# Recurrence of a two-block transformer on one core: block-diagonal products as pairs of array tiles

## The chip, the cores and the metric

The kernel runs on one core of a Trainium2 chip. The metric is device time in microseconds: the median of three runs was 2415.47 us (2414.92 to 2416.41). Besides these runs one execution was profiled, with 2423.21 us; its instructions span 2421.4 us. All rows below are of that execution.

## The reference, cut to what matters

The program is a stack of two blocks on 256 tokens of width 1024, all in float32. The first block's first token mixer is a bidirectional RWKV-7: 16 heads of width 64, a forward and a backward direction, and per head and direction the recurrence

```
state = state * w_t + sa * b_t + v_t * k_t        # state 64 x 64, sa = state . a_t
y_t   = state . r_t
```

over the 256 tokens. Everything before it (norms, projections, decay and gate) and everything after it (group norm of y, output projection, mixture of experts with 32 experts, then a dilated attention, a second mixture of experts, and a second model with two layers of its own) is not touched by the change.

## The kernel before

The recurrence is computed in chunks of 64 tokens. A job is one direction (z) and two heads (hp = 0, 1), named by et = 0 to 7; so there are 16 jobs, each with 2 heads x 4 chunks. Two chunks lie side by side on the 128 partitions: chunk c = 2 tt + cp, with cp = 0 on partitions 0 to 63 and cp = 1 on 64 to 127 (`rows(cp)`). The pair of a head and of a pair of chunks is q = 2 hp + tt. A tile such as `mq[:, q, s]` is 128x128 and block-diagonal: a 64x64 block for cp = 0 in the upper left, one for cp = 1 in the lower right, and zeros elsewhere. MQB (four such matrices per q), LGK (three) and ZZ are set to zero once, and only the diagonal blocks are written later.

A job goes through these steps; after each `yield` the next generator gets its turn:

- L1113: inner products of b, k with a, r, one 64x64 array tile per head and chunk; each head has a PSUM tile of its own (`psa[hp]`). VectorE multiplies them by masks into MQB (L1119) and LGK (L1121); L1123 puts inverses of 16x16 blocks into `mq[:, :, 1]`.
- Twice (lv = 0, 1), to extend the inverse from blocks of 16 to 32 and then 64: transposes of `mq[:, q, 1]` (L1137), copied by ScalarE into Mt (L1141); product of `mq[:, q, 0]` and Mt (L1147); VectorE masks it into Z (L1149); product of Z and `mq[:, q, 1]` (L1167); VectorE adds it (L1169). At lv = 0 there are also transposes (L1155, L1175), the product of `lg_[:, q, 0]` and v (L1162), and ScalarE's copies of them (L1156, L1164, L1178).
- L1183: the inverse times AW, four products of 128x128 by 128x128 into one PSUM tile; ScalarE copies the result to UW (L1186).
- L1194 and L1198, "the last ones": UW times `mq[:, q, 2:4]` (i = 1 into pw, i = 0 into py) and v times `lg_[:, q, 1:3]` added into py. The contraction runs over both chunks, and since the right-hand matrices are block-diagonal a product has 256 columns: s = 0, 1 times two chunks. VectorE adds pw into RA (L1202, L1203); ScalarE copies py to YH (L1205).
- Then `across` starts as a generator of its own: the state goes from chunk to chunk (L1221 transpose, L1223 copy, L1226 product, L1229 and L1230 adds), and at its end `norm` is appended after every second et.

`roundrobin` takes turns between two chains of jobs (one per direction, each with its own MQB, LGK, SB and ZZ), the `across` and `norm` generators, and `side`, which loads and multiplies the modulation weights of both layers (L1849, products of 128x32 array tiles by 512 columns). PSUM has two tags of four tiles each ("b", "c"), a tile being one bank. The order of the instructions on each engine comes from this order of emission and from the framework's scheduler, which can bring an independent instruction forward. Every f32 product shows as two records in the profile, a transpose as one.

When the recurrence is done, `tail` opens more buffers for weights, and the loads of the output projection and of the experts follow.

Of the kernel before, what the change touches and what calls it, by code (L numbers as in the profile page):

```python
# [20 lines left out]
F32 = mybir.dt.float32  # L21
F32R = mybir.dt.float32r
I32 = mybir.dt.int32
AF = mybir.ActivationFunctionType
OP = mybir.AluOpType
AX = mybir.AxisListType
P = 128
# [677 lines left out]
def rwkv(N, src, I, cst, emit, side, tail, scratch):  # L705


    nc, tc = N.nc, N.tc
    v, g, sc = nc.vector, nc.gpsimd, nc.scalar
# [4 lines left out]
    rows = lambda h: slice(h * 64, h * 64 + 64)  # L714
# [13 lines left out]
    o = 0  # L728
# [41 lines left out]
    for tt in range(NT):  # L770
        src.norm(tt)
        for k4 in range(2):
            ps = N.psum("b")
            for kk in range(4):
                nc.tensor.transpose(ps[:, kk * P:(kk + 1) * P], src.tok(tt, 4 * k4 + kk), N.ident)
            o, pk = hc[:, 4 * k4:4 * k4 + 4, tt * P:(tt + 1) * P], ps.rearrange("p (k t) -> p k t", k=4)
# [55 lines left out]
    for i, dst in ((0, hw), (1, ha)):  # L832
        xs = shifted(3 + i)
        ps = N.psum("b")
# [10 lines left out]
    ps = N.psum("b")  # L845
# [179 lines left out]
    jp = pool("jp", 2, e4s)  # L1025
# [65 lines left out]
    def job(z, et, buf):  # L1091
# [3 lines left out]
        ar = AR[z][e2].rearrange("p s (c t) -> p s c t", t=64)[:, :, 4 * e:4 * e + 4]  # L1095
        pl = PL[z][e2][:, 4 * e:4 * e + 4]
        vz = vt[:, :, et * P:(et + 1) * P]
        if z:
            vz = jp.tile([P, NT, P], F32, tag="vr", name=N.nm("vr"))
            ps = N.psum("c")  # L1100
# [2 lines left out]
            sc.activation(vz, ps[:, 0:256].rearrange("p (t x) -> p t x", t=2), AF.Copy)  # L1103
        mq, lg_, sb = MQB[buf], LGK[buf], SB[buf]
        t4 = lambda a: a.rearrange("p (q t) -> p q t", q=4)
        pairs = [(hp, tt) for hp in range(2) for tt in range(2)]
        psa = [N.psum("b") for _ in range(2)]
        for i, src in ((0, bt), (1, kt)):
            for tt in range(2):
                for hp in range(2):  # L1110
                    for cp in range(2):
                        c = 2 * tt + cp
                        nc.tensor.matmul(psa[hp][rows(cp), (2 * i + tt) * P:(2 * i + tt + 1) * P], c3(src)[rows(hp), c, :],  # L1113
                                         ar[rows(hp), 0:2, c, :], start=True, stop=True)
        for hp in range(2):
            for cp in range(2):
                a = psa[hp][rows(cp), :].rearrange("p (i t s x) -> p i t s x", i=2, t=2, s=2)
                o = mq[rows(cp), 2 * hp:2 * hp + 2, 0::2, cp * 64:cp * 64 + 64]
                v.tensor_mul(o, a[:, 0], m_ni[rows(cp), None, :, :].to_broadcast([64, 2, 2, 64]))  # L1119
                o = lg_[rows(cp), 2 * hp:2 * hp + 2, 0:2, cp * 64:cp * 64 + 64]  # L1120
# [10 lines left out]
        DP = jp.tile([P, 4, 64], F32, tag="DP", name=N.nm("DP"))  # L1131
        g.tensor_mul(DP, eye[:, None, :].to_broadcast([P, 4, 64]), pb)
        AW = jp.tile([P, 4, 2, 64], F32, tag="AW", name=N.nm("AW"))
        for lv in range(2):
# [5 lines left out]
            Mt = jp.tile([P, 4, 64], F32, tag="Mt", name=N.nm("Mt"))  # L1140
# [3 lines left out]
            qbc = lambda a: a.rearrange("p (q b c) -> p q b c", q=4, c=sz)  # L1144
            pz = N.psum("b")
            for q in range(4):
                nc.tensor.matmul(pz[:, q * 64:(q + 1) * 64], mq[:, q, 0, :], Mt[:, q, :], start=True, stop=True)  # L1147
            Z = ZZ[buf][:, lv]
            v.tensor_mul(Z.rearrange("p q (b s c) -> p q s b c", s=2, c=sz)[:, :, 0], qbc(pz[:, 0:256]),  # L1149
                         blk(m_lv[lv], 0)[:, None].to_broadcast([P, 4, 64 // sz, sz]))  # L1150
# [1 line left out]
            if lv == 0:  # L1152
                ps = N.psum("c")
                for tt in range(2):
                    nc.tensor.transpose(ps[:, tt * P:(tt + 1) * P], at[:, tt * P:(tt + 1) * P], N.ident)  # L1155
                sc.activation(AW[:, :, 1, :].rearrange("p (h t) d -> p t h d", h=2),  # L1156
                              ps[:, 0:256].rearrange("p (t h d) -> p t h d", t=2, h=2), AF.Copy)
                pc = N.psum("c")
                for q, (hp, tt) in enumerate(pairs):
                    vh = vz[:, tt, hp * 64:(hp + 1) * 64]  # L1160
                    for cp in range(2):
                        nc.tensor.matmul(pc[rows(cp), q * 64:(q + 1) * 64], lg_[:, q, 0, cp * 64:cp * 64 + 64], vh,  # L1162
                                         start=True, stop=True)
                sc.activation(AW[:, :, 0, :], c3(pc[:, 0:256]), AF.Copy)  # L1164
            pm = N.psum("b")
            for q in range(4):
                nc.tensor.matmul(pm[:, q * 64:(q + 1) * 64], Z[:, q, :], blk(mq[:, q, 1, :], 1), start=True, stop=True)  # L1167
            o = mq[:, :, 1, :].rearrange("p q (b s c) -> p q s b c", s=2, c=sz)[:, :, 1]
            v.tensor_add(o, o, qbc(pm[:, 0:256]))  # L1169
            yield  # L1170
# [9 lines left out]

        pu = N.psum("b")
        for q in range(4):
            nc.tensor.matmul(pu[:, q * P:(q + 1) * P], mq[:, q, 1, :], AW[:, q].rearrange("p s d -> p (s d)"), start=True,  # L1183
                             stop=True)
        UW = jp.tile([P, 4, 2, 64], F32, tag="Z", name=N.nm("UW"))
        sc.activation(UW, pu.rearrange("p (q s d) -> p q s d", q=4, s=2), AF.Copy)  # L1186
        yield

        pw, py = N.psum("c"), N.psum("b")
        for tt in range(2):  # L1190
            for i, ps in ((1, pw), (0, py)):
                for hp in range(2):
                    q = 2 * hp + tt
                    nc.tensor.matmul(ps[rows(hp), tt * 256:(tt + 1) * 256], UW[:, q, i, :], mq[:, q, 2:4, :], start=True,  # L1194
                                     stop=i == 1)
            for hp in range(2):
                q = 2 * hp + tt
                nc.tensor.matmul(py[rows(hp), tt * 256:(tt + 1) * 256], vz[:, tt, hp * 64:(hp + 1) * 64],  # L1198
                                 lg_[:, q, 1:3, :], start=False, stop=True)
        RA = jp.tile([P, 2, 2, 2, 64], F32, tag="RA", name=N.nm("RA"), bufs=3)  # L1200
        w5 = pw.rearrange("p (t s c x) -> p t s c x", t=2, s=2, c=2)
        v.tensor_add(RA[:, :, 0], w5[:, :, 0], ar[:, 1].rearrange("p (t c) x -> p t c x", t=2))  # L1202
        v.tensor_add(RA[:, :, 1], w5[:, :, 1], DP.rearrange("p (t c) x -> p t c x", t=2))  # L1203
        YH = jp.tile([P, 2, 2, 2, 64], F32, tag="YH", name=N.nm("YH"), bufs=3)
        sc.activation(YH, py.rearrange("p (t s c x) -> p t s c x", t=2, s=2, c=2), AF.Copy)  # L1205
        gens.append(across(z, et, buf, RA, YH))
        yield

# [979 lines left out]
```

## Time and profile before

| | |
|---|---|
| median of 3 runs | 2415.47 us |
| profiled execution | 2423.21 us |
| its span | 2421.4 us |
| TensorE busy (share of span) | 2112.9 us (87%) |
| VectorE busy | 1151.2 us (48%) |
| ScalarE busy | 704.8 us (29%) |
| GpSimd busy | 369.3 us (15%) |
| mean granted TensorE clock | 0.92 |

Busy times are unions over the whole span, which has stages with different limits. TensorE's matmul records (PE) have modelled ends and overlap each other, and weight loads (PEld) run beside them; the pace of a queue is read from the starts. The granted clock is a share of full speed.

### The profile page before, as it was taken

How to read it: one execution, taken by the hardware profiler on the slowest of the kernel's cores; microseconds unless marked ns; L12 is line 12 of the kernel's file. 1: busy time of each engine (PE TensorE's matmuls, PEld its weight loads, DVE VectorE, ACT ScalarE, POOL GpSimd, SP SyncE). 2: the span in 40 equal slices, each digit the busy share in tenths (PEclk: the TensorE clock that was granted, in tenths of full speed). 3: DMA queues.
4: the chain of work that ended last, by engine and by line, in shares of the span. 5: the costliest groups of instructions: out<-in, count | busy, mean ns of one | idle time of the engine just before them, and what ended most of it. 6: DMA issues, size and time to landing. Idle time of an engine off the chain costs nothing. (4 is left out here: it accounts for less than half of the span.)

```text
span 2421.4 us, 37833 instructions
## 1 busy us (share of the span) xinstructions
PE 2112.9 (87%) x15008; PEld 1508.4 (62%) x15008; DVE 1151.2 (48%) x2567; ACT 704.8 (29%) x1261; POOL 369.3 (15%) x300
## 2 busy tenths in 40 slices
PE   4987799997997699999898799988997799979896
PEld 2864477765654398997654377766564577766552
DVE  5777666766331344437332166663231575652132
ACT  2432133333110244434111034531121245521120
POOL 1144102222000121121000022220010222210010
PEclk8986799998998799999999789998999799989997
DMA  8424623147899754344999944367999544469996
GB/s 270 141 90 144 217 93 112 62 144 280 347 416 419 297 190 156 122 157 176 357 418 419 375 134 148 131 239 312 415 413 409 207 139 136 159 266 404 414 402 273
DMA packets 162985, 605.86 MB, mean 250 GB/s; under 512 B 36960, under 2 KB 37984, under 8 KB 107488
## 3 DMA queue, kind: packets, MB, share of 16 engines
q1 hardware_dynamic: 159072, 599.64, 65.3%
q0 software_dynamic: 3136, 3.16, 0.6%
q8 instruction: 124, 2.03, 0.3%
q10 hardware_dynamic: 576, 0.39, 0.1%
q14 instruction: 77, 0.63, 0.1%
HBM read 602.09 MB, written 1.05 MB: 249 GB/s over the span
## 5 line engine op out<-in xcount | busy, mean ns | idle before, releaser
L360 PE MATMUL psb<-w,xg 128*32 128x256 f32 (+1 forms) x4096 | 394.4, 433 | 89.8 <-DMA w<-in_moe_w_up_dram 29.5
L360 PEld LDWEIGHTS psb<-w,xg 128*32 128x32 f32 (+1 forms) x4096 | 214.0, 135 | 279.8 <-issue 70.7
L562 ACT ACTIVATE wh<-w 128x1024 fp32r<-128x1024 f32 x230 | 240.6, 1060 | 287.5 <-PE psb L652 149.8
L566 POOL TENSOR_TENSOR wl<-w,wh 128x1024 fp32r<-128x1024 f32 x80 | 198.7, 2485 | 585.0 <-ACT wh L562 464.5
L566 DVE TENSOR_TENSOR wl<-w,wh 128x1024 fp32r<-128x1024 f32 x150 | 200.5, 1343 | 168.1 <-ACT wh L562 139.3
L420 DVE SCALAR_TENSOR_TENSOR hid<-psb,gs,sg 128x256 f32<-128x256 f32 x44 | 30.0, 681 | 401.1 <-PE psb L360 401.1
L651 PE MATMUL psb<-wh,xh 128*128 128x512 f32 x448 | 185.9, 416 | 4.0 <-ACT wh L562 2.4
L652 PE MATMUL psb<-wh,xl 128*128 128x512 f32 x448 | 182.0, 407 | 0.3 <-DVE xl L143 0.3
L360 PE MATMUL psb<-w,hT 128*32 128x512 f32 (+1 forms) x1024 | 167.2, 597 | 5.3 <-DMA w<-in_moe_w_down_dram 2.2
L649 PE MATMUL psb<-wl,xh 128*128 128x512 f32 x448 | 130.4, 398 | 3.2 <-POOL wl L566 1.7
L142 ACT ACTIVATE yh<-psb 128x512 fp32r<-128x512 f32 x88 | 52.5, 597 | 227.7 <-DVE psb L441 126.9
L1849 PE MATMUL psb<-w,c_fm 128*32 128x512 f32 x384 | 87.0, 759 | 33.3 <-DMA w<-in_ada_w_dram 29.7
L143 DVE TENSOR_TENSOR yl<-psb,yh 128x512 fp32r<-128x512 f32 x88 | 60.9, 692 | 98.5 <-ACT yh L142 98.5
L360 PE MATMUL psb<-pm,xh 128*128 128x256 f32 (+1 forms) x384 | 102.6, 303 | 4.3 <-DVE pm L343 4.3
L360 PEld LDWEIGHTS psb<-w,hT 128*32 128x32 f32 (+1 forms) x1024 | 46.4, 119 | 92.5 <-issue 74.4
L404 ACT ACTIVATE pt<-psb 128x256 fp32r<-128x256 f32 x44 | 16.9, 384 | 297.7 <-PE psb L360 297.7
L651 PEld LDWEIGHTS psb<-wh,xh 128*128 128x128 f32 x448 | 87.0, 194 | 24.3 <-ACT wh L562 3.6
L649 PEld LDWEIGHTS psb<-wl,xh 128*128 128x128 f32 x448 | 85.2, 192 | 23.2 <-POOL wl L566 2.5
L360 PE MATMUL psb<-pm,xl 128*128 128x256 f32 (+1 forms) x384 | 99.0, 293 | 0.0
L652 PEld LDWEIGHTS psb<-wh,xl 128*128 128x128 f32 x448 | 87.3, 195 | 18.5 <-DVE xl L143 1.2
L620 PE MATMUL psb<-axh,wh 128*128 128x256 f32 x384 | 93.7, 282 | 0.0
L620 PE MATMUL psb<-axl,wh 128*128 128x256 f32 x384 | 93.7, 282 | 0.0
(575 smaller groups left out, 3906.5 us busy)
## 6 DMA issues: line engine op xcount, KB each, us to landing
w<-in_moe_w_gate_dram SPq DMA_DIRECT2D x64, 1024.0 KB, 18.5
w<-in_moe_w_up_dram SPq DMA_DIRECT2D x64, 1024.0 KB, 18.2
w<-in_moe_w_down_dram SPq DMA_DIRECT2D x64, 1024.0 KB, 19.8
w<-in_w_exp_up_dram SPq DMA_DIRECT2D x64, 1024.0 KB, 12.6
w<-in_w_exp_gate_dram SPq DMA_DIRECT2D x64, 1024.0 KB, 9.4
w<-in_w_exp_down_dram SPq DMA_DIRECT2D x64, 1024.0 KB, 16.9
w<-in_ada_w_dram SPq DMA_DIRECT2D x48, 1024.0 KB, 5.2
w<-in_w_in_dram SPq DMA_DIRECT2D x44, 1024.0 KB, 5.1
```

The costliest lines, as they stand in the source:

```text
L142: self.nc.scalar.activation(hi, src, AF.Copy)
L143: (eng or self.nc.vector).tensor_sub(lo, src, hi.bitcast(F32))
L360: keep(nc.tensor.matmul(*a, **k))
L404: nc.scalar.activation(pt[g], ps[:, 0:256], AF.Copy)
L420: v.scalar_tensor_tensor(hid[g].rearrange("s j p -> s p j"), pu[:, :256].rearrange("s (p j) -> s p j", j=2), gs[g], sg.rearrange("s (p j) ...
L562: nc.scalar.activation(wh, w, AF.Copy)
L566: i = (nc.gpsimd if eng == "g" else nc.vector).tensor_sub(wl, w, wh.bitcast(F32))
L620: mm = lambda a, b, **f: nc.tensor.matmul(o, a[:, kk, ws], b[:, k, :], skip_group_check=True, **f)
L649: nc.tensor.matmul(pss[tt], xh[:, k, t], wl[:, kk, :], start=False, stop=k == nk - 1)
L651: nc.tensor.matmul(pss[tt], xh[:, k, t], wh[:, kk, :], start=k == 0, stop=False)
L652: nc.tensor.matmul(pss[tt], xl[:, k, t], wh[:, kk, :], start=False, stop=False)
L1849: nc.tensor.matmul(ps[32 * j:32 * j + 32, :], self.c[:, k:k + 1].to_broadcast([P, 32]), wt[:, j * 512:(j + 1) * 512], start=k == 0, stop=k ...
```

## The change

Products whose left or right matrix is block-diagonal are issued per chunk, on the 64 partitions and the 64 columns of that chunk's block, with the result on the same 64 partitions (L1147, L1162, L1167, L1183). One product of 128x128 weights becomes two of 64x64. For the last ones each product is also split by chunk: 24 products of 64x64 weights by 128 columns per job in place of 12 of 128x64 by 256. The results of chunk cp, both for RA and for YH, go to one PSUM tile `pb_[cp]`: columns 0 to 255 are y, columns 256 to 511 w. The adds into RA and the copy into YH are split by chunk too: four adds of 128x128 in place of two of 128x256, two copies of 128x256 in place of one of 128x512.

```diff
--- before.py
+++ after.py
@@ -1103,6 +1103,7 @@
             sc.activation(vz, ps[:, 0:256].rearrange("p (t x) -> p t x", t=2), AF.Copy)
         mq, lg_, sb = MQB[buf], LGK[buf], SB[buf]
         t4 = lambda a: a.rearrange("p (q t) -> p q t", q=4)
+        chunk = lambda a, cp: a[rows(cp), cp * 64:cp * 64 + 64]
         pairs = [(hp, tt) for hp in range(2) for tt in range(2)]
         psa = [N.psum("b") for _ in range(2)]
         for i, src in ((0, bt), (1, kt)):
@@ -1144,7 +1145,8 @@
             qbc = lambda a: a.rearrange("p (q b c) -> p q b c", q=4, c=sz)
             pz = N.psum("b")
             for q in range(4):
-                nc.tensor.matmul(pz[:, q * 64:(q + 1) * 64], mq[:, q, 0, :], Mt[:, q, :], start=True, stop=True)
+                for cp in range(2):
+                    nc.tensor.matmul(pz[rows(cp), q * 64:(q + 1) * 64], chunk(mq[:, q, 0], cp), Mt[rows(cp), q], start=True, stop=True)
             Z = ZZ[buf][:, lv]
             v.tensor_mul(Z.rearrange("p q (b s c) -> p q s b c", s=2, c=sz)[:, :, 0], qbc(pz[:, 0:256]),
                          blk(m_lv[lv], 0)[:, None].to_broadcast([P, 4, 64 // sz, sz]))
@@ -1157,14 +1159,15 @@
                               ps[:, 0:256].rearrange("p (t h d) -> p t h d", t=2, h=2), AF.Copy)
                 pc = N.psum("c")
                 for q, (hp, tt) in enumerate(pairs):
-                    vh = vz[:, tt, hp * 64:(hp + 1) * 64]
                     for cp in range(2):
-                        nc.tensor.matmul(pc[rows(cp), q * 64:(q + 1) * 64], lg_[:, q, 0, cp * 64:cp * 64 + 64], vh,
-                                         start=True, stop=True)
+                        nc.tensor.matmul(pc[rows(cp), q * 64:(q + 1) * 64], chunk(lg_[:, q, 0], cp),
+                                         vz[rows(cp), tt, hp * 64:(hp + 1) * 64], start=True, stop=True)
                 sc.activation(AW[:, :, 0, :], c3(pc[:, 0:256]), AF.Copy)
             pm = N.psum("b")
             for q in range(4):
-                nc.tensor.matmul(pm[:, q * 64:(q + 1) * 64], Z[:, q, :], blk(mq[:, q, 1, :], 1), start=True, stop=True)
+                for cp in range(2):
+                    nc.tensor.matmul(pm[rows(cp), q * 64:(q + 1) * 64], chunk(Z[:, q], cp), blk(mq[:, q, 1, :], 1)[rows(cp)], start=True,
+                                     stop=True)
             o = mq[:, :, 1, :].rearrange("p q (b s c) -> p q s b c", s=2, c=sz)[:, :, 1]
             v.tensor_add(o, o, qbc(pm[:, 0:256]))
             yield
@@ -1180,29 +1183,32 @@
 
         pu = N.psum("b")
         for q in range(4):
-            nc.tensor.matmul(pu[:, q * P:(q + 1) * P], mq[:, q, 1, :], AW[:, q].rearrange("p s d -> p (s d)"), start=True,
-                             stop=True)
+            for cp in range(2):
+                nc.tensor.matmul(pu[rows(cp), q * P:(q + 1) * P], chunk(mq[:, q, 1], cp),
+                                 AW[rows(cp), q].rearrange("p s d -> p (s d)"), start=True, stop=True)
         UW = jp.tile([P, 4, 2, 64], F32, tag="Z", name=N.nm("UW"))
         sc.activation(UW, pu.rearrange("p (q s d) -> p q s d", q=4, s=2), AF.Copy)
         yield
 
-        pw, py = N.psum("c"), N.psum("b")
+
+        pb_ = [N.psum("c"), N.psum("b")]
+        RA = jp.tile([P, 2, 2, 2, 64], F32, tag="RA", name=N.nm("RA"), bufs=3)
+        YH = jp.tile([P, 2, 2, 2, 64], F32, tag="YH", name=N.nm("YH"), bufs=3)
         for tt in range(2):
-            for i, ps in ((1, pw), (0, py)):
-                for hp in range(2):
-                    q = 2 * hp + tt
-                    nc.tensor.matmul(ps[rows(hp), tt * 256:(tt + 1) * 256], UW[:, q, i, :], mq[:, q, 2:4, :], start=True,
-                                     stop=i == 1)
-            for hp in range(2):
-                q = 2 * hp + tt
-                nc.tensor.matmul(py[rows(hp), tt * 256:(tt + 1) * 256], vz[:, tt, hp * 64:(hp + 1) * 64],
-                                 lg_[:, q, 1:3, :], start=False, stop=True)
-        RA = jp.tile([P, 2, 2, 2, 64], F32, tag="RA", name=N.nm("RA"), bufs=3)
-        w5 = pw.rearrange("p (t s c x) -> p t s c x", t=2, s=2, c=2)
-        v.tensor_add(RA[:, :, 0], w5[:, :, 0], ar[:, 1].rearrange("p (t c) x -> p t c x", t=2))
-        v.tensor_add(RA[:, :, 1], w5[:, :, 1], DP.rearrange("p (t c) x -> p t c x", t=2))
-        YH = jp.tile([P, 2, 2, 2, 64], F32, tag="YH", name=N.nm("YH"), bufs=3)
-        sc.activation(YH, py.rearrange("p (t s c x) -> p t s c x", t=2, s=2, c=2), AF.Copy)
+            for i in (1, 0, 2):
+                for cp in range(2):
+                    for hp in range(2):
+                        q = 2 * hp + tt
+                        o = pb_[cp][rows(hp), (i % 2) * 256 + tt * P:(i % 2) * 256 + (tt + 1) * P].rearrange("p (s x) -> p s x", s=2)
+                        a = vz[rows(cp), tt, hp * 64:(hp + 1) * 64] if i == 2 else UW[rows(cp), q, i, :]
+                        b = (lg_[rows(cp), q, 1:3] if i == 2 else mq[rows(cp), q, 2:4])[:, :, cp * 64:cp * 64 + 64]
+
+                        nc.tensor.matmul(o, a, b, start=i == 1 and tt == 0, stop=i > 0, skip_group_check=True)
+        for cp in range(2):
+            py, pw = (pb_[cp][:, i * 256:(i + 1) * 256].rearrange("p (t s x) -> p t s x", t=2, s=2) for i in range(2))
+            v.tensor_add(RA[:, :, 0, cp], pw[:, :, 0], ar[:, 1].rearrange("p (t c) x -> p t c x", t=2)[:, :, cp])
+            v.tensor_add(RA[:, :, 1, cp], pw[:, :, 1], DP.rearrange("p (t c) x -> p t c x", t=2)[:, :, cp])
+            sc.activation(YH[:, :, :, cp], py, AF.Copy)
         gens.append(across(z, et, buf, RA, YH))
         yield
```

## Rows read from the trace of the kernel before

**Rows 1.** Windows of the recurrence: busy time and count per engine, clock, DMA.

```profile
core 0: us, PE busy (x) PEld busy (x) DVE busy (x) ACT busy (x) POOL busy (x), PEclk, DMA share, GB/s
300.00:500.00 200.00, 195.69 (x1908) 147.03 (x1904) 135.25 (x355) 74.68 (x209) 37.94 (x59) 0.97 0.26 86
500.00:540.00 40.00, 37.75 (x290) 25.29 (x286) 25.04 (x72) 15.76 (x44) 11.07 (x16) 1.00 0.44 147
```

**Rows 2.** Lines L1113, L1198: ns min/median/max, first and last start.

```profile
L1113 PE MATMUL psb<-ar,bk x512: 269/269/470, 264.8 to 499.9; 64*64 64x128 f32 x171
...
L1198 PE MATMUL psb<-LGK,vr x64: 379/379/379, 301.6 to 530.1; 128*64 128x256 f32 x64
```

**Rows 3.** Time line of TensorE, one pair: start, us, merged records, idle before.

```profile
334.22 1.10 PE L1113 MATMUL psb<-ar,bk 64*64 64x128 f32 x32
...
335.25 0.52 PEld L1102 LDWEIGHTS psc<-vt,cm 128*128 128x128 f32 x4 [0.17 <-issue]
...
345.35 0.69 PE L1162 MATMUL psc<-vt,LGK 128*64 128x64 f32 x16
...
345.35 0.55 PEld L1162 LDWEIGHTS psc<-vt,LGK 128*64 128x64 f32 x16 [0.34 <-ACT ST L1223]
...
353.76 0.97 PEld L1147 LDWEIGHTS psb<-Mt,MQB 128*128 128x128 f32 x8 [0.67 <-ACT Mt L1141]
...
355.10 1.87 PEld L1167 LDWEIGHTS psb<-MQB,ZZ 128*128 128x128 f32 x16
...
357.28 1.86 PEld L1183 LDWEIGHTS psb<-AW,MQB 128*128 128x128 f32 x16
...
359.75 0.60 PE L1194 MATMUL psb<-MQB,UW 128*64 128x256 f32 x4
...
360.18 0.60 PE L1198 MATMUL psb<-LGK,vt 128*64 128x256 f32 x4
...
364.59 1.10 PE L1113 MATMUL psb<-ar,bk 64*64 64x128 f32 x32
```

**Rows 4.** Time line of SyncE's queue: load issues behind the recurrence.

```profile
531.54 4.22 SPq L78 DMA_DIRECT2D w<-in_rw_w_o_dram  x3
535.81 0.50 SPq L78 DMA_DIRECT2D w<-in_moe_w_gate_dram  x1
```

**Rows 5.** Lines by form, 262 to 540: busy us, mean ns, idle before.

```profile
L1147 PE MATMUL psb<-Mt,MQB 128*128 128x64 f32 x256 | 35.0, 280 | 1.1 <-ACT Mt L1141 1.1
...
L1113 PE MATMUL psb<-ar,bk 64*64 64x128 f32 x512 | 24.5, 294 | 0.0
...
L1141 ACT ACTIVATE Mt<-psc 128x256 f32<-128x256 f32 x32 | 11.9, 381 | 17.8 <-PE psc L1137 17.1
...
L1230 DVE TENSOR_TENSOR Y<-psc,YH 128x64 f32<-128x64 f32 x48 | 10.3, 223 | 1.1 <-PE psc L1226 0.3
...
L1205 ACT ACTIVATE YH<-psb 128x512 f32<-128x512 f32 x16 | 9.6, 597 | 33.8 <-PE psb L1198 23.7 <-issue 5.7 <-POOL Y L1215 4.3
...
L1202 DVE TENSOR_TENSOR RA<-psc,ar 128x256 f32<-128x256 f32 x16 | 6.7, 421 | 12.3 <-PE psc L1194 12.3
```

**Rows 6.** Windows of 5 us in the recurrence, columns as in rows 1.

```profile
337.00:342.00 5.00, 5.00 (x45) 3.54 (x46) 4.88 (x14) 1.32 (x4) 0.00 (x0) 1.00 0.60 208
...
347.00:352.00 5.00, 4.30 (x47) 3.75 (x46) 4.70 (x12) 2.79 (x8) 0.00 (x0) 1.00 0.84 298
...
437.00:442.00 5.00, 3.77 (x33) 3.06 (x32) 3.94 (x14) 1.31 (x4) 0.88 (x1) 0.77 0.47 190
442.00:447.00 5.00, 5.00 (x35) 4.55 (x35) 1.68 (x5) 0.77 (x2) 2.80 (x2) 0.50 0.00 0
447.00:452.00 5.00, 4.56 (x28) 4.09 (x27) 3.80 (x11) 3.65 (x11) 1.17 (x2) 0.71 0.26 52
```

**Rows 7.** Waits, 262 to 540 us: total us, times, longest.

```profile
DVE MQB L1169 <- PE psb L1167: 33.8, 30, 2.5
...
DVE ZZ L1149 <- PE psb L1147: 30.4, 19, 3.8
```

## The prediction

> **What bounds the kernel now.** The views were read in this order: the page, the recurrence's stretch by windows, its instructions by line and form, its time line, its waits, the clock, and the transfers behind it. The page has TensorE busy 87% of the span, but only the stage that the change edits decides. From 300 to 500 us TensorE is busy 195.7 of 200 us, VectorE 135.3 and ScalarE 74.7 [rows 1]. The reader is to see that TensorE is the limit there and VectorE, with 68%, stands right behind it. The stage runs from the first L1113 (264.8 us) to the last L1198 (about 530) [rows 2]: 16 jobs, two at a time, so eight pairs; from the timeline one pair takes 364.59 - 334.22 = 30.4 us [rows 3]. DMA is at 26% of its time there [rows 1], and the loads for the next stage are issued when the recurrence has ended (531 us) [rows 4], so what is saved in the stage should move everything behind it forward one to one. I take that transfer as whole.
>
> **Prices per record.** The profile shows each f32 product as two records (16 jobs x 2 levels x 4 products = 128 products, 256 records at L1147 [rows 5]). Mean durations (280 ns) are latencies; what counts in a queue is the distance between starts, read from the merged rows of [rows 3]:
> - Loading 128 columns of weights: L1167, 16 records, (1.87 - 0.19)/15 = 0.112 us each, although only 64 columns stream; L1183 with 128 columns streaming has the same 0.111. So the weight load sets the pace of both.
> - 64 columns loaded, 256 streaming, 128 rows deep: L1194 to L1198, 0.43 us for 4 records = 0.1075. That is 0.42 ns a column, or 0.0538 for 128 columns, 0.027 for 64.
> - 64 columns loaded, 64 streaming (L1162): (0.69 - 0.24)/15 = 0.030, the loads' row (0.55 - 0.15)/15 = 0.027.
> - 64x64 tiles, 128 columns streaming (L1113): 32 records, (1.10 - 0.27)/31 = 0.027, half of 0.0538. So products of the two row halves run at once there, each half into a bank of its own.
>
> **The change part by part.**
> - L1147 and L1167: 8 records of 0.111 (0.89 us) become 16 that load and stream 64 columns: 16 x 0.027 = 0.43. Gain 0.46, 64 groups (32 at each line): 29.4 us. It does not need two halves to run at once, since 0.027 is also the serial price for 64 columns.
> - L1162: same records, half as deep. No row of [rows 3] has a pace under 0.027, so 0.027 before and after: nothing.
> - L1183: 8 x 0.111 = 0.89 becomes 16 records with 128 columns. Between 0.43 (as L1113) and 16 x 0.0538 = 0.86 (serial). No row shows two row halves that write one bank, though different partitions of it. I take 0.43, since L1113 is the same shape: 0.46 x 16 = 7.4; the other end is 0.03 x 16 = 0.5.
> - The last ones: 24 records of 0.1075 (2.58 us) become 48 of 128 columns. The order (two columns of tiles, then the other rows) and the two banks, one per row half, are those of L1113: 48 x 0.027 = 1.29, gain 1.29 x 16 = 20.6. The other end, 48 x 0.0538 = 2.58, is no gain.
> - Sum on TensorE: 57.4 us, lower bound 29.9.
>
> What takes from it:
> - Changes of tile form. Where the form changes a row shows 0.17 us of "issue" (L1102 after L1113) [rows 3]. In the time line between the first and the last of those rows I count 16 changes, and 21 with the new forms (L1147 between transposes costs both ways; L1162 to L1167, L1183 to the last ones and to the next L1113 no longer change). 5 x 0.17 x 8 = 6.8 us.
> - New waits behind shortened work. First, at 353.76 L1147 of the second job already waits 0.67 us for its Mt from ScalarE [rows 3], so the first job's 0.46 there only lengthens that wait. Second, UW (ACT, 0.60 us) of the first job lies under the second job's L1183 (0.89); with 0.43 left as cover TensorE waits about 0.45, and behind it in the queue are all 48 records, and RA and YH for them. Third, from 337 to 342 us VectorE is busy 4.88 of 5 us with the masks of L1119 and L1121 [rows 6]; of the 0.92 that L1147 saves next to it I count half as wait. 0.46 + 0.45 + 0.46 = 1.37 per pair, 11 us in all.
> - VectorE and ScalarE. Two adds of 128x256 (0.42 us) [rows 5] become four of 128x128, by an estimate midway to L1230's 0.22 [rows 5] 0.31 each: 0.4 us more per job. YH in halves adds 0.16 by the rows of 256 and 512 columns, 0.38 and 0.60 [rows 5]. Both lie beside the next pair's 64 records at L1113 (1.7 us), and I count nothing. If that cover goes, it is 0.8 per pair, 6 us. VectorE then has 0.68 x 30.4 + 0.8 = 21.4 us of work in a pair of about 26: near the limit, not over it.
> - The clock. After a gap at TensorE (busy 3.77 of 5 us from 437 us) the granted clock fell to 0.50, the lower of its two levels (1.2 against 2.4 GHz), and came back only near 450 [rows 6]; ten such microseconds cost five. The mean of 0.97 from 300 to 500 us [rows 1] is 6 us lost, 12 at the lower level, so this one fall is nearly all of it. With more waits I count one more: 5 us.
>
> Sum against the profiled execution (2423.2 us, span 2421.4): -57.4 + 6.8 + 11 + 5 = -34.6, so 2388.6. The median of the runs shown is 2415.5, 7.7 lower, and the same saving gives 2381 us.
>
> One rule of the Trainium skill speaks against a term. What the rows show is above: L1113's row halves overlap with a bank each, and none shows a shared bank [rows 3]. The Trainium skill, page "TensorEngine Tiling (Array Packing)", section "Restrictions and Gotchas", says that different row tiles write to different banks and cannot use the same one at the same time. By that rule L1183 would be serial, which is the third rival, and L1147, L1162 and L1167 would stay at 0.027.
>
> **The rivals.**
> - All of it arrives: TensorE stays the limit, the round robin of two jobs and the side work fills each wait. -57.4 + 6.8 = -51, 2365 us. For it: TensorE busy 97.8% [rows 1]. Against it: VectorE already ends many waits, 33.8 us before L1169 and 30.4 before L1149 [rows 7], and TensorE's own waits are short only because its queue is long.
> - Only the loads get shorter: the last ones run serially in spite of their banks, L1183 too. UW keeps its cover then, and two waits of 0.46 in eight pairs, 7.4, are left: -29.9 + 6.8 + 7.4 = -16, 2400 us. For it: nothing in L1113, which has the same shape; it differs in that the last ones accumulate.
> - One bank shared is serial (the rule above): L1183's 6.9 us are missing, -28, 2388 us. As likely as not by the rows, but small.
> - The clock eats it: a gap in each pair's VectorE run, and the lower level for 10 us each time. Seven dips more cost 35 us: -57.4 + 6.8 + 11 + 35 = -5, 2411 us. For it: the dip at 437 us is one of just these places [rows 6]. Against it: at 347 us TensorE was busy only 4.30 of 5 and kept its clock [rows 6].
> - Slower: in a shared bank each change of row half waits until the product before it has left the array. Place: L1147, L1162, L1167 and L1183, 96 groups of 8 changes. Price: one record's whole latency, 0.29 us as L1113's mean [rows 5], so 8 x 0.29 = 2.3 us a group: 80 groups at 2.3 - 0.89 and the 16 of L1162 at 2.3 - 0.43 are +143; less 20.6 from the last ones, plus 6.8, +129 or 2544 us. The point from which it decides: 0.05 us a change (96 x 8 x 0.05 = 38) cancels the -39.6 that the sum has without the clock. Against it: L1113, with a bank for each row half, shows no cost at its changes.
>
> **How the numbers follow.** Forecast (stalls eat a third) 0.47, all of it 0.15, one bank serial 0.12, loads only 0.10, clock 0.09, slower 0.07. The predicted time is 2381 us. The range has to take in 2365 and 2400 and their spread of some 6 us: 2359 to 2409, which leaves out the slower case, most of the clock case and small parts of the others, some 2 in 10. A measurement of this kernel tells 0.2% (4.8 us) from no change. Faster by more: all but the slower case and half of the clock case, less a little: 0.86. Within: 0.05, from the clock case. Slower: 0.09.
>
> **What would show it.** L1147's and L1167's successors: 16 records in about 0.55 us of loads in place of 0.97 for 8. The last products of a job: 48 records in about 1.3 us. L1183's successor: 0.43 or 0.86 us tells whether a shared bank is serial. A pair's period near 26 us instead of 30.4. TensorE's waits for UW and Mt larger, VectorE's before ZZ smaller. Stretches at clock 0.50 between 300 us and the stage's end: more than two would make the gain too large in my sum. The prediction is wrong if the stage shortens by under 10 us, or if the stage shortens and the stage of the experts starts no earlier.

## The result and the profile after

The changed kernel takes 2392.15 us (median of 6 runs, 2386.19 to 2402.28) against 2418.14 us (6 runs, 2414.92 to 2422.92; the three reported above are among them) of the kernel before: ratio 0.9887 with a 95% interval of 0.9865 to 0.991, so 22 to 33 us faster. In a later session (experiment 8) it was 0.992 (0.9898 to 0.9942). The forecast was 34.6 us. The sign was right, and about three quarters of the size arrived. The two largest savings came at about the size forecast; one smaller saving failed, and one wait that the forecast counted as nothing appeared. The profile after is of the slowest of its runs (2402.28 us, span 2400.5 us).

The lines moved by one to eight: L1113 is now L1114, L1141 L1142, L1147 L1149, L1162 L1163, L1167 L1169, L1183 L1187, L1186 UW L1190; the last ones (L1194, L1198) are all L1206, RA L1209 and L1210, YH L1211.

The stage, from the changed kernel's windows (they answer to [rows 1]; the second is its own steady part):

```profile
core 0: us, PE busy (x) PEld busy (x) DVE busy (x) ACT busy (x) POOL busy (x), PEclk, DMA share, GB/s
300.00:500.00 200.00, 185.30 (x2888) 135.75 (x2882) 151.10 (x417) 83.59 (x244) 44.28 (x70) 0.95 0.32 109
...
302.10:477.90 175.80, 161.74 (x2594) 120.21 (x2595) 135.18 (x374) 73.27 (x214) 33.45 (x55) 0.95 0.30 104
```

and from the first and last starts of L1114 and L1206 and the first load issues behind (they answer to [rows 2, 4]):

```profile
L1114 PE MATMUL psb<-ar,bk x512: 269/269/473, 267.1 to 477.9; 64*64 64x128 f32 x171
```

```profile
L1206 PE MATMUL psb<-LGK,vr x64: 269/269/269, 297.6 to 504.9; 64*64 64x128 f32 x64
```

```profile
506.26 4.42 SPq L78 DMA_DIRECT2D w<-in_rw_w_o_dram  x3
510.73 0.50 SPq L78 DMA_DIRECT2D w<-in_moe_w_gate_dram  x1
```

The stage now lasts 504.9 - 267.1 = 237.8 us, where it was 265.3, and the loads behind it are issued 25.3 us earlier. So the gain lies in the stage and is passed on; what follows the stage took 1895.6 us in this profile and 1891.3 before, with code that the change does not touch. TensorE, idle for 4.3 of 200 us before [rows 1], is idle for 175.80 - 161.74 = 14.1 us of the steady part, and the clock fell from 0.97 to 0.95.

TensorE's time line of one pair answers to [rows 3]:

```profile
298.42 0.39 PE L1114 MATMUL psb<-ar,bk 64*64 64x128 f32 x4
299.31 0.89 PE L1114 MATMUL psb<-ar,bk 64*64 64x128 f32 x24 [0.50 <-ACT YH L1211]
...
316.62 0.68 PE L1149 MATMUL psb<-Mt,MQB 64*64 64x64 f32 x16
...
319.46 1.15 PE L1169 MATMUL psb<-MQB,ZZ 64*64 64x64 f32 x32
...
321.12 1.96 PE L1187 MATMUL psb<-AW,MQB 64*64 64x128 f32 x32
322.92 0.32 PE L1206 MATMUL psc<-MQB,UW 64*64 64x128 f32 x2
...
325.49 0.28 PE L1206 MATMUL psb<-LGK,vr 64*64 64x128 f32 x2
325.58 0.38 PE L1114 MATMUL psb<-ar,bk 64*64 64x128 f32 x4
326.47 0.78 PE L1114 MATMUL psb<-ar,bk 64*64 64x128 f32 x20 [0.50 <-ACT YH L1211]
```

The reader is to see four things. A pair takes 325.58 - 298.42 = 27.2 us in place of 30.4. The last ones of two jobs, 96 records, take 325.58 - 322.92 = 2.66 us, 0.028 each, as predicted. L1149 and L1169 go at (0.68 - 0.22)/15 = 0.031 and (1.15 - 0.23)/31 = 0.030 a record. L1187 goes at (1.96 - 0.27)/31 = 0.0545: its 16 records a job take 0.87 us, what the eight of L1183 took. And L1114 waits behind its first four records for YH, which it never did before. The waits of the stage, answering to [rows 7] and to the waits in [rows 3, 5]:

```profile
PEld psb L1114 <- ACT YH L1211: 8.6, 9, 2.2
PEld psb L1149 <- ACT Mt L1142: 8.2, 9, 1.1
PE psb L1114 <- ACT YH L1211: 6.5, 9, 1.9
PE psb L1149 <- ACT Mt L1142: 4.0, 5, 1.0
```

```profile
DVE ZZ L1151 <- PE psb L1149: 20.2, 17, 3.1
DVE MQB L1172 <- PE psb L1169: 18.0, 22, 1.8
```

(total us, times, longest; the PEld rows are the wait of the weight loads, the PE rows that of the matmuls, which counts as TensorE's idle time here.) VectorE waits less for TensorE (38.2 us against 64.2), and TensorE more for ScalarE. Where the wait for YH comes from is seen in the time line of all engines around 325 us:

```profile
324.69 0.28 DVE L1210 TENSOR_TENSOR RA<-psc,DP 128x128 f32<-128x128 f32 x1
324.89 0.28 DVE L1209 TENSOR_TENSOR RA<-psb,ar 128x128 f32<-128x128 f32 x1
325.07 0.38 ACT L1211 ACTIVATE YH<-psc 128x256 f32<-128x256 f32 x1 [1.34 <-DVE RA L1210]
325.09 0.28 DVE L1210 TENSOR_TENSOR RA<-psb,DP 128x128 f32<-128x128 f32 x1
...
325.49 0.52 ACT L1223 ACTIVATE SB<-YH 64x64 f32<-64x64 f32 x2
...
326.03 0.38 ACT L1211 ACTIVATE YH<-psb 128x256 f32<-128x256 f32 x1
...
326.47 1.09 PE L1114 MATMUL psb<-ar,bk 64*64 64x128 f32 x28 [0.50 <-ACT YH L1211]
```

Before the change RA's and YH's products had a bank each: VectorE read the one, ScalarE the other. Now each bank holds both for one chunk, ScalarE's YH follows VectorE's two RA adds on the same bank, the second chunk's YH stands behind two SB copies too, and only then is a "b" bank free for the next job. The Trainium skill, page "PSUM — Partial Sum Buffer", section "PSUM bank collisions raise a hardware error", says that two engines may not touch one bank and quadrant at once, reads included, and that the program must order them. The order in this trace agrees: YH starts 0.10 us after the RA add on its bank has ended, though it reads other columns.

A gap can cost more than itself. The granted clock fell three times in this stage after 300 us, to the lower of its two levels (1.2 against 2.4 GHz): at 355 us, behind two waits for YH of 0.61 and 0.80 us; at 420 us, during a wait of 1.81 us for Y, which VectorE makes; and at 471 us, behind the longest wait for YH, 1.93 us:

```profile
420.95 0.45 PE L1227 MATMUL psc<-ident,SB 128*128 128x128 f32 x1 [1.81 <-DVE Y L1236]
...
468.21 0.38 PE L1114 MATMUL psb<-ar,bk 64*64 64x128 f32 x4
470.52 1.09 PE L1114 MATMUL psb<-ar,bk 64*64 64x128 f32 x28 [1.93 <-ACT YH L1211]
```

```profile
470.00:475.00 5.00, 4.48 (x49) 0.67 0.02 5
475.00:480.00 5.00, 5.00 (x24) 0.50 0.00 0
480.00:485.00 5.00, 5.00 (x54) 0.81 0.64 210
```

(start, us and idle before; then, in windows of 5 us behind the last of the three, TensorE's busy time, its clock and the DMA's share and rate). 5 x (0.33 + 0.50 + 0.19) = 5.1 us went behind a wait of 1.9. Such waits need not bring a fall: two of 0.62 and 0.80 us at 413 and 414 us were followed by a clock of 1.00 up to 420 us, and the fourth experiment shows the same for longer ones.

### The profile page after: what moved, and what is told of

The parts are those of the page before. It is cut to its first block, busy times and chain, and to the rows that moved or that the text cites. A ratio compares the mean times of both kernels' runs of the same rounds, so it can differ in the third digit from the quotient of the medians.

```text
span 2400.5 us, 39938 instructions
## 1 busy us (share of the span) xinstructions
PE 2077.4 (87%) x16032; PEld 1482.2 (62%) x16032; DVE 1154.3 (48%) x2599; ACT 707.3 (29%) x1277; POOL 366.4 (15%) x300
## 5 line engine op out<-in xcount | busy, mean ns | idle before, releaser
L360 PE MATMUL psb<-w,hT 128*32 128x512 f32 (+1 forms) x1024 | 173.3, 609 | 8.4 <-DMA w<-in_moe_w_down_dram 3.9
## 6 DMA issues: line engine op xcount, KB each, us to landing
w<-in_w_exp_up_dram SPq DMA_DIRECT2D x64, 1024.0 KB, 13.2
w<-in_w_exp_gate_dram SPq DMA_DIRECT2D x64, 1024.0 KB, 10.3
```

Source lines behind the costliest of these rows:

```text
L360: keep(nc.tensor.matmul(*a, **k))
```

## The experiments

Each expectation was on record before its run. Ratios are to the kernel before on the same chip. The table at the end of the section splits every profile's stage.

**1. The last ones alone.** The kernel before, with only the last ones as in the change.

```
-        pw, py = N.psum("c"), N.psum("b")
+        pb_ = [N.psum("c"), N.psum("b")]
...
+            for i in (1, 0, 2):
+                for cp in range(2):
```

> Only the last ones are split by chunk (48 records of 64x64 tiles, one bank per chunk); L1147, L1162, L1167 and L1183 stay as before. Theory A (the trace of the changed kernel: the last ones overlap at 0.027 us a record, 20.6 us of TensorE's time, and the next job's L1113 waits for YH's copy out of the shared bank, 8 to 9 us of that): 12 us less than before, and waits of L1113 for ACT YH of 5 to 9 us in the trace. Rival B (VectorE is the limit of the stage already, with four adds into RA in place of two): 0 to 4 us less, or slower.

Measured: 2419.42 us, ratio 0.9988 (0.9978 to 0.9999), only 3 us faster. The saving at the records was there, and lost: L1114's weight loads waited 11.5 us for YH, and the clock was 0.95 in the steady part and 0.93 in the last job (0.97 and 1.00 before). Theory A had forecast 12 us; 3 us lies in the range of rival B, that four adds make VectorE the limit. The ninth experiment, which has the same four adds, decides against B.

```profile
PEld psb L1114 <- ACT YH L1207: 11.5, 9, 2.2
```

**2. The blocks alone.** L1147, L1162, L1167 and L1183 as in the change, the last ones as before.

> Only L1147, L1162, L1167 and L1183 are issued per block; the last ones, RA and YH stay as before. Theory A: the shorter weight loads of L1147 and L1167 are worth 29 us of TensorE's time and L1183 nothing (its two row halves write one bank one after the other); less 5 us for more changes of tile form and some waits for Mt: 15 to 20 us less than before, and no wait of L1113 for YH. Rival B (VectorE is the limit): under 10 us less. If the two halves' gains simply add, this run and the one with the last ones alone together make 26 us; if they hide each other, each alone brings nearly as much as both.

Measured: 2404.79 us, ratio 0.993 (0.9913 to 0.9947), 17 us faster, and no wait of L1114 for YH in the trace. This half of the sum was right. With the 3 us of the first experiment that makes 20, where both halves together make 22 to 33: the intervals don't tell whether the halves simply add.

**3. The two banks of the last ones swapped.** The changed kernel; the first chunk, whose RA and YH come first, now has the "b" bank.

```
-        pb_ = [N.psum("c"), N.psum("b")]
+        pb_ = [N.psum("b"), N.psum("c")]
```

> The changed kernel with the two tags exchanged: chunk 0 of the last ones writes a bank of tag b, chunk 1 one of tag c, so that the b bank, which the next job's L1113 wants, is copied out about 1 us earlier. Theory A (TensorE's idle time before L1113, 0.74 us in each of 9 places, is the wait for YH's second copy behind two copies into SB on ScalarE): that wait goes, 4 to 7 us less than the changed kernel, a ratio to before of 0.985 to 0.987. Rival C (the wait only moves: the next c bank, for L1102 or the transposes, is late by as much): the same as the changed kernel, 0.989, with a new wait of L1102 or L1137's successor for YH.

Measured: 2386.48 us, ratio 0.9865 (0.9844 to 0.9886). The interval overlaps that of the changed kernel (0.9865 to 0.991), so the 5 us between them are not shown by this run alone. The wait of the weight loads fell from 8.6 to 3.1 us, and the clock was 0.99 and 1.00 in the stage:

```profile
PEld psb L1114 <- ACT YH L1211: 3.1, 4, 1.2
```

TensorE's idle time in the steady part fell only from 14.1 to 12.2 us, so part of this wait was replaced by others.

**4. L1187's products in two banks.** The two 64x64 blocks that follow each other write different banks, and UW is read in two halves. It asks whether the shared bank makes them serial, the prediction's third rival.

```
-        pu = N.psum("b")
+        pu = [N.psum("b") for _ in range(2)]
...
+                r = (q + 2 * cp) % 4
-                nc.tensor.matmul(pu[rows(cp), q * P:(q + 1) * P], chunk(mq[:, q, 1], cp),
+                nc.tensor.matmul(pu[r // 2][rows(cp), (r % 2) * P:(r % 2 + 1) * P], chunk(mq[:, r, 1], cp),
...
```

> The changed kernel with L1183's products in two banks and in an order in which the two row halves write different banks at any time (q = 0 for chunk 0 beside q = 2 for chunk 1, and so on); UW is copied in two halves of 256 columns. Theory D (a shared bank makes row halves serial): L1183's successor falls from 0.0545 us a record to 0.027, 0.43 us a job; the time is 3 to 5 us less than the changed kernel, as UW's copy then has less cover. Rival E (tiles on the diagonal do not overlap, whatever the bank): it stays at 0.0545 and the time does not change, or grows by the second copy.

Measured: 2390.56 us, ratio 0.9872 (0.985 to 0.9894). The pace of the records did not change: (1.96 - 0.27)/31 = 0.0545 us each, as in the changed kernel, and 0.051 by the weight loads, far from 0.027:

```profile
346.51 1.96 PE L1188 MATMUL psb<-AW,MQB 64*64 64x128 f32 x32
346.51 1.72 PEld L1188 LDWEIGHTS psb<-AW,MQB 64*64 64x64 f32 x32 [0.17 <-DVE MQB L1172]
```

So the bank is not the reason, and the explanation by the bank falls. Pace and time came as rival E had them (tiles on the diagonal do not overlap), whose reason the next experiment tests. The new explanation was this: a record streams a column in about 0.85 ns in its own tile, and different tiles run side by side. Four 64x64 tiles then give 0.027 us per record of 128 columns (L1113), two give 0.0545 whatever their banks (L1187), and a lone one would give 0.109.

This trace also has the changed kernel's waits of the weight loads for YH (8.3 us, 9 times). At two places where the changed kernel waited 1.81 and 1.93 us and its clock fell, this one waited 1.81 and 1.58 us, and its clock stayed at 1.00:

```profile
420.66 0.30 PE L1229 MATMUL psc<-ident,SB 128*128 128x128 f32 x1 [1.81 <-DVE Y L1238]
467.97 1.09 PE L1114 MATMUL psb<-ar,bk 64*64 64x128 f32 x28 [1.58 <-ACT YH L1213]
```

```profile
420.00:425.00 5.00, 3.83 (x74) 1.00 0.01 3
470.00:475.00 5.00, 5.00 (x49) 1.00 0.15 28
```

**5. Nine forms of product side by side.** It measures the disputed price by itself.

```
+        for i in range(16):
+            r, c, bank = tiles[i % len(tiles)]
...
+                tc.keep_in_program_order(nc.tensor.matmul(ps[bank][rows(c), q * P:q * P + wide],
+                                                          m0[rows(r), q, 0, c * 64:c * 64 + 64], m0[rows(r), q, 1, 0:wide],
...
```

> The kernel before, with rows of products put in at the start of the recurrence, 16 products (32 records, a weight load and a matmul each) to a form, in program order: full 128x128 by 128 columns (five times, the first four to bring the clock up); one lone 64x64 tile by 128 columns; two tiles of the same rows in one bank; two tiles of the same columns in two banks; the diagonal pair in one bank; the diagonal pair in two banks; all four tiles, a bank per row half; the diagonal pair in one bank by 64 columns; one lone tile by 64 columns. Its time as a whole says nothing. Theory (two different tiles run side by side, whatever their bank): per record at 128 columns the full form about 0.11 us, the lone tile 0.109, each of the four pairs 0.054, four tiles 0.027; at 64 columns the diagonal pair 0.027 and the lone tile 0.054. Rival (a shared bank makes the diagonal pair serial): the lone tile and the diagonal pair in one bank both 0.054, the diagonal pair in two banks 0.027, at 64 columns in one bank 0.027 for the pair and 0.027 for the lone tile. Second rival (only tiles of different rows run side by side): the pair of the same rows goes at the lone tile's pace, the pair of the same columns at half of it.

Measured, one window of half a microsecond inside each form, in the order of the text (busy time, records that touch the window, clock, DMA):

```profile
284.50:285.00 0.50, 0.50 (x7) 1.00 0.00 0
287.50:288.00 0.50, 0.50 (x7) 1.00 0.00 0
289.50:290.00 0.50, 0.50 (x14) 1.00 0.00 0
291.50:292.00 0.50, 0.50 (x15) 1.00 0.00 0
293.00:293.50 0.50, 0.50 (x14) 1.00 0.00 0
295.00:295.50 0.50, 0.50 (x14) 1.00 0.00 0
296.00:296.50 0.50, 0.50 (x28) 1.00 0.00 0
297.00:297.50 0.50, 0.50 (x25) 1.00 0.00 0
298.50:299.00 0.50, 0.50 (x12) 1.00 0.00 0
```

A record lasts 0.27 us (0.22 with 64 columns), so a pace p puts (0.50 + 0.27)/p of them into a window: 7 is 0.11 us, 14 is 0.055, 28 is 0.0275. The full product and the lone tile go at 0.11. All four pairs go at half of it: same rows, same columns, diagonal in one bank, diagonal in two. Four tiles go at a quarter. With 64 columns the diagonal pair has (0.50 + 0.22)/25 = 0.029 and the lone tile 0.06. Every form came out by the new explanation, and both rivals fall, and with them rival E of the fourth experiment: the diagonal pair takes half of what the lone tile takes. No form goes below 0.027, so whether a record could be faster than that is not shown. The records of 64x64 tiles make one merged row of the time line:

```profile
285.39 14.30 PE L1048 MATMUL psb<-MQB 64*64 64x128 f32 x255
```

Less one latency that is 14.0 us, and the prices give 32 x (0.109 + 4 x 0.0545 + 0.027 + 0.027 + 0.0545) = 13.9.

The Trainium skill's rule that the prediction weighed ("TensorEngine Tiling (Array Packing)", "Restrictions and Gotchas": different row tiles cannot use one bank at the same time) shows no price here, and the measurement decides: the diagonal pair, two row tiles that write different partitions of the bank, goes at the same pace in one bank or two. Two row tiles that write the same partitions of one bank were not tried.

**6. L1183 as before.** The swapped variant, with one 128x128 product per pair of chunks there again.

```
-            for cp in range(2):
-                nc.tensor.matmul(pu[rows(cp), q * P:(q + 1) * P], chunk(mq[:, q, 1], cp),
+            nc.tensor.matmul(pu[:, q * P:(q + 1) * P], mq[:, q, 1, :], AW[:, q].rearrange("p s d -> p (s d)"), start=True,
...
```

> The variant that swaps the two banks of the last ones, but with the product M1 by (A - A') ahead of them as one 128x128 product per pair of chunks again, as in the kernel before. Theory (the two 64x64 blocks by 128 columns each cost together what one 128x128 product costs, 16 records at 0.054 against 8 at 0.11): the time of the swapped variant within 0.2%, 2384 to 2390 us, and the product's row lasts 0.9 us as before. Rival (the blocks do save the 7.4 us that the prediction gave them, and it is lost behind them): the row lasts as long but TensorE's idle time beside it changes, and the time differs by over 3 us.

Measured: 2388.71 us, ratio 0.9876 (0.9856 to 0.9896), against 0.9865 with the blocks: no difference that these runs can tell. The two jobs' products last as long as the blocks' 1.96 us:

```profile
317.71 1.95 PE L1186 MATMUL psb<-AW,MQB 128*128 128x128 f32 x16
```

So TensorE gains nothing from this part of the change, where the prediction gave it 7.4 us. It is the rows that decide this; the two intervals alone would leave room for several us.

**7. The LGK copies on VectorE.** The swapped variant; of the four copies per job behind L1178, the two into LGK go from ScalarE to VectorE.

```
-                        sc.activation(dst[rows(cp), :, cp * 64:cp * 64 + 64].rearrange("p (h t) d -> p t h d", h=2),
...
+                        if i:
+                            v.tensor_copy(od, pd)
+                        else:
+                            sc.activation(od, pd, AF.Copy)
```

> The swapped variant, with the second of the two copies per job from PSUM into LGK on VectorE instead of ScalarE, so that ScalarE reaches Mt earlier. Theory (what is left of the new idle time of TensorE in this stage is ScalarE's, above all the wait for Mt ahead of the products by the inverse): that wait falls from about 8 us to under 4, and the time falls by 4 to 8 us against the swapped variant, to 2379 to 2383 us. Rival (VectorE, busy for some 80% of the stage, is late instead: ZZ and MQB come later by the 0.3 us of each copy, 32 copies of it on the path): no gain, or up to 8 us slower, with the waits for VectorE grown by as much as the wait for ScalarE falls.

Measured: 2380.05 us, ratio 0.9851 (0.9827 to 0.9874), 8.7 us by the medians and 6 by the ratios under the sixth kernel, which has the same swap, on the same chip (the ends of the two intervals overlap). The wait for Mt is all but gone (8.2 us in the swapped variant, 0.7 here), VectorE is busy 141.3 of 161.6 us, and it has become no worse a limit: TensorE's waits for SB and Y, which VectorE makes, are 1.1 us each from 300 to 495 us (0.9 and 2.4 in the swapped variant). The theory held for Mt. The wait for YH, though, is 5.7 us here, against 3.1 in the swapped variant and 4.1 in the sixth kernel.

```profile
L1149 PEld LDWEIGHTS psb<-Mt,MQB 64*64 64x64 f32 x512 | 18.0, 137 | 6.8 <-issue 3.8 <-ACT Mt L1142 0.7
```

**8. The changed kernel again**, beside the two before.

> The changed kernel once more, on the chip of the other runs, to have it beside the swapped variant's kin. Theory (TensorE waits for YH because the first bank of the last ones is the one that the next job's first products take): 5 to 7 us slower than the variants that swap the two banks, with 6 to 9 us of waits of the first products for YH that those lack. Rival (the swap's gain was the clock's or the chip's): the same time as those within 0.1%.

Measured: 2396.85 us, ratio 0.992 (0.9898 to 0.9942), 8 us behind the sixth kernel, which has the swap and, without effect on TensorE, L1183 as before; the intervals just do not overlap. The waits of L1114 for YH were 8.0 us from 300 to 495 us, there 4.1. The swap's gain is not the chip's.

**9. The last ones alone, with swapped banks.** The first experiment with the third one's edit.

> The kernel before with the last ones alone changed (as in the first experiment), and with the two banks swapped, so that the first chunk's products go to the bank that the next job's first products need and that one comes free first. Theory (the saving of 20.6 us at the last ones was lost to the first products' wait for YH, 11.5 us, and to the clock after it): the wait falls to under 4 us, the granted clock from 300 us on comes back to 0.97 or more, and the time is 12 to 18 us under the kernel before, ratio 0.9925 to 0.995. Rival (the last ones alone bring nothing, since another engine sets a pair's period as long as the products ahead of them are unchanged): 0 to 5 us under it, ratio 0.998 to 1, though the wait for YH is gone.

Measured: 2406.87 us, ratio 0.9935 (0.9921 to 0.9949), 15 us faster in place of 3. The wait fell to 5.3 us, not under 4, and the profiled run, the slowest of its five, had the clock at 0.96. So the order of the banks ate most of the first experiment's gain, 12 us of it; the intervals are far apart.

**10. SB copies on GpSimd.** The seventh kernel, with the two SB copies moved off ScalarE, ahead of GpSimd's own copy into Y.

```
+            g.tensor_copy(sb[rows(hp), hp * 64:hp * 64 + 64], YH[rows(hp), 0, 1, 0])
-            sc.activation(sb[rows(hp), hp * 64:hp * 64 + 64], YH[rows(hp), 0, 1, 0], AF.Copy)
```

> The variant with swapped banks and one LGK copy on VectorE, and with the two small copies of YH into SB (0.26 us each on ScalarE, between the first job's YH copies and the second job's) on GpSimd instead. Theory (what is left of the first products' wait for YH, 5.7 us in that variant, is ScalarE's queue): the wait falls to 2 to 4 us, and the time by 1 to 4 us more, ratio to the kernel before 0.983 to 0.985. Rival (GpSimd takes far longer over such a copy than ScalarE, and the transposes of SB behind it come later): no gain, ratio 0.985 to 0.988, with new waits of the transposes for GpSimd.

Measured: 2380.35 us, ratio 0.9837 (0.9822 to 0.9852). The interval overlaps the seventh's, so whether it is faster is not settled. The wait for YH hardly moved, from 5.7 to 5.2 us: the theory falls, ScalarE's queue is not what is left of it. The first part of the rival's reason falls too: GpSimd took 0.249 us a copy by the profile, as ScalarE's 0.255 (spans on GpSimd are rough). Its second part came, though small: the transposes' weight loads now wait 2.7 us for GpSimd's SB, where they waited 2.2 us for ScalarE's. This or the seventh is the fastest version found, by the ratios some 36 to 40 us under the kernel before.

```profile
PEld psc L1231 <- POOL SB L1226: 2.7, 3, 1.4
```

**Where each stage's time is.** Length from the first L1114 to the last of the last ones; TensorE's idle time in the steady part (from 35 us after the stage's start to the last L1114); what the lower clock took, (1 - clock) x length, with the last job; and the rest: TensorE's records, its changes of form, and idle time and clock of the first 35 us (11.8 us together before, 10.9 in the changed kernel). The clock has two digits, so its column is good to about 1 us. Each row is one execution.

| kernel | stage | idle | clock | rest |
|---|---|---|---|---|
| before | 265.3 | 4.3 | 6.0 | 255.0 |
| changed | 237.8 | 14.1 | 10.7 | 213.0 |
| changed, again (8) | 236.1 | 12.8 | 8.6 | 214.7 |
| last ones alone (1) | 263.3 | 13.8 | 12.0 | 237.5 |
| the same, swapped (9) | 259.2 | 9.6 | 7.9 | 241.7 |
| blocks alone (2) | 246.4 | 9.4 | 3.7 | 233.3 |
| swapped (3) | 227.5 | 12.2 | 1.7 | 213.6 |
| two banks at L1187 (4) | 234.1 | 13.9 | 1.7 | 218.5 |
| L1183 as before (6) | 229.1 | 13.2 | 3.4 | 212.5 |
| LGK on VectorE (7) | 222.5 | 9.3 | 1.6 | 211.6 |
| SB on GpSimd (10) | 222.1 | 9.0 | 3.2 | 209.9 |

The rest is 213 to 215 us for the changed and the swapped kernel, so those differ in idle time and clock alone. In these profiles it is the clock above all: 9 of the 10.3 us between the changed and the swapped one, 5.2 of the 7.0 between the eighth kernel and the sixth. But the profiles are not typical. The changed kernel's is its slowest run, with a mean clock over the whole span of 0.915 (the other five 0.918 to 0.926); the swapped one's is its fastest, with 0.931 (the other three 0.922 to 0.924). And the fourth kernel, with the changed one's waits for YH, lost 1.7 us to the clock. So how much of the swap's gain is the clock's, and what decided whether the clock fell, stays open.

## Why the prediction was right, and where it was not

- **L1147 and L1167 (29.4 us).** Right in size: 0.030 to 0.031 us a record gives 0.48 us a group, where the forecast had 0.43; that saves 26 us. The reason was wrong. "It does not need two halves to run at once, since 0.027 is also the serial price" took L1194's 0.42 ns a column [rows 3] for one tile's own pace. L1194 goes to two column tiles in turn; a lone tile pays twice that (experiment 5). The saving needs the two blocks to run side by side, which they do.
- **L1183 (7.4 us).** Failed; the other end, 0.5 us, was nearer. The step that failed is "I take 0.43, since L1113 is the same shape". L1113 keeps four tiles busy, a diagonal pair two, and two tiles by 128 columns are what one full product costs. "So the weight load sets the pace of both" holds for L1167, which streams 64 columns; at L1183 it is not shown, since a lone tile that loads 64 columns and streams 128 takes 0.109 us too (experiment 5). The prediction had the right outcome among its rivals, but for a reason (the bank) that experiments 4 and 5 exclude.
- **The last ones (20.6 us).** Right at the records: 48 x 0.0277 = 1.33 us against 2.58, 20 us.
- **Changes of form (6.8 us).** The stage's rest fell by 255.0 - 213.0 = 42 us, and the records' savings are 26 + 20 to 29 + 21, so the changes took some 4 to 8 us, if nothing else in the rest changed. The time line has 22 and 21 of them in two pairs of the changed kernel, as the forecast counted (21), and 16 and 18 in two pairs before; their price was not measured by itself.
- **Waits (11 us).** Idle time grew by 9.8 us: the size was right, the place half wrong. The wait for Mt grew as forecast, from 3.8 to 8.2 us on the weight loads and from 1.1 to 4.0 on the matmuls. No wait for UW is in the trace: L1187 did not get shorter and keeps covering it. The third forecast wait, for VectorE's masks at L1147, is 0.2 us on the matmuls. In their place stands the wait for YH, 6.5 us on the matmuls. The step that failed is "Both lie beside the next pair's 64 records at L1113 (1.7 us), and I count nothing": RA and YH do not lie beside those records, which need the bank that RA and YH read. The prediction had priced the loss of that cover at 6 us and left it out of the sum. Their durations were right (adds of 0.28 us against the estimated 0.31; YH 0.38).
- **The clock (5 us).** 4.7 us more in this profile, with three falls in place of one, more than the two that the prediction named as its limit. Luck had a part in this match: the kernel again (8) lost 8.6 us, 2.6 more than before, and the fourth kernel, with the same waits for YH, 1.7.
- **Sum.** -(46 to 50) + 6.8 + 9.8 + 4.7 = -25 to -29; the stage measured -27.5 and the runs -26. The 6.8 in this sum is the forecast's own term, and its measured counterpart is what the stage left over, so the sum closes in part by construction. What the forecast had too much is L1183's 7.4 us, and some 3 at L1147 and L1167. That the waits came out near 11 us was partly chance, as one forecast wait was absent and an unforeseen one took its room.

The slower rival (2.3 us at every change of row half in one bank) and the one with serial last ones are excluded by the paces; "all of it arrives" failed by TensorE's 10 us of new idle time. The one in which the clock eats the gain needed seven more dips; the trace has two more.

## What to carry to other kernels

Count how many tiles of the array are busy at once, not how many columns are loaded: two diagonal blocks streaming as many columns as the full product gain nothing, and gain half only where the load of the weights, not the streaming, had set the pace. When the layout of PSUM changes, follow each bank to its last reader and to the next product that wants it; in this kernel two engines that read one bank followed each other, and the chunk that is read first belongs into the bank that is wanted first. Behind a saving on TensorE look for the next ScalarE copy on the path: moving two of a job's small copies to VectorE, though it was busy for 80% of the stage, brought 6 to 9 us, about as much as the swap.

## What was not expected of the hardware

- 64x64 tiles in f32: 0.109 us for 128 columns in one tile, the same as a full 128x128 product; 0.055 with any two tiles at once; 0.0275 with four. Which two, and in one bank or two for a diagonal pair, made no difference.
- The order of two banks moved the kernel by about 8 us (experiments 6 and 8), and by 12 with the last ones alone (1 and 9). How much of this went through the clock is open: one wait of 1.93 us was followed by 5.1 us lost at the lower level, while waits of 1.81 and 1.58 us in the fourth kernel were followed by none.
- GpSimd copied 64x64 f32 within SBUF in 0.249 us by its rough spans, ScalarE in 0.255.
